# Where a layer's merge gates run: eight of sixteen moved from the Mamba stage to the end of the HGRN2 heads

## The chip, the cores and the metric

One core of a Trainium2 chip runs the whole program in one launch. The metric is device microseconds, the median of several executions.

## What is computed

One layer of a streaming encoder for two groups of requests that share the weights: a prompt of 512 tokens, and 8 sampled streams of 16 tokens. Normalised and modulated tokens `h` go through one wide projection, and its parts feed two mixers side by side, a gated linear attention (HGRN2) and a state space model (Mamba-2). Two of the parts, `ga` and `gb`, gate the mixers' outputs:

```python
proj = h @ w_in
q_r, f_r, i_r, g_r, z, xbc, dt_r, ga_r, gb_r = jnp.split(proj, cuts, axis=-1)
...
o = (_rms(o) * hg_norm_w.astype(f32).reshape(HG_HEADS, HG_DV)).reshape(bn, t, HG_WIDTH)
o = (o * jax.nn.silu(g_r.astype(f32))).astype(h.dtype)
pa = o @ w_branch_a
...
pb = y @ w_branch_b
merged = jax.nn.sigmoid(ga_r) * pa + jax.nn.sigmoid(gb_r) * pb
```

`ga` and `gb` have 1024 columns each, so they are sixteen column blocks of 128. Behind the mixers come `w_out`, a second norm and an expert channel mixer (PEER), which takes the larger part of the time and is not touched by the change.

## The kernel before

The tokens are worked on in two passes that share weight loads: A (names that end in A; the first 128 prompt tokens and the 128 sampled ones, 256 columns) and B (384 prompt tokens). Values lie transposed, channels on partitions. A projection of one block of 128 output channels is float32 made of three matmuls per block of 128 input channels (`mm3`, L265): `wsplit` (L255) loads 512 KB of weights as `raw` on SP's queue, ScalarE rounds it to `whi` and VectorE takes the rest as `wlo`; then 24 matmuls of 128x256 (pass A) go to one PSUM bank of the kind `pj`. There are four such banks, three banks `sm` for everything else, and one `ad`. The rings of the weights have 5 (`raw`) and 4 (`whi`, `wlo`) buffers.

The stages, in the order of the program:

- `hgrn_in` (L572): four head pairs. Each has its V projections for both passes (L588), three projections for each of its two heads and both passes (`projs`, L295), and then `hgrn_head` (L626) for pass A's two heads: the levels of the attention (L649), the state (L672), the sample streams (L686, L698), and at the end the output: a copy to the tile `oT` (L704), its square, a column sum on TensorE, Ln and Exp for the norm (L312, L313), two multiplications (L708 and the one ahead of it) and a store (L709). `oT` has two buffers in the pool of this stage. After the third pair the dt projections of both passes are made (`steps_all`).
- `mamba_in` (L806): first GA = 4 gates, then four groups. A group (`mamba_out`, L833) has six projections with convolutions (ScalarE copies the bank to `xp`, L784) and four for z, then `mamba_group` (L853): transposes, the state (L892) and outputs, a norm at the end. Behind each group come GG = 3 gates.
- `merge` (L969) loads the gates and both mixers' outputs back from DRAM.

A gate (`gate`, L827) is one projection, a Sigmoid on ScalarE into the tile `stGA` (two buffers, in a pool that is opened when the heads are through) and a store to `g_sp` on ScalarE's queue. The change touches the constants GA and GG, `hgrn_in`, `mamba_in` and `gate`.

`projs` also advances a generator (`step`, L308) that spreads the rest of the ada projections (the conditioning, L495: four matmuls a step into the `ad` bank; L501 puts the finished result in place) over the projections of these stages.

The program is written in this order, but each engine's order is then set by the framework's scheduler, which simulates the program and may move an instruction ahead of others on its engine:

```python
with tile.TileContext(nc, schedule_with_timeline_sim=True) as tc, ExitStack() as ctx:
```

So an instruction of a later stage can stand among those of an earlier one, where its tiles and banks allow it.

Of the kernel before, what the change touches and what calls it, by code (L numbers as in the profile page):

```python
# [8 lines left out]
F32 = mybir.dt.float32  # L9
# [8 lines left out]
P = 128  # L18
# [110 lines left out]


LATE = 0
GA = 4
GG = 3
GS = 0
L2 = 10
L3 = 0
# [54 lines left out]
class Kernel:  # L191
# [380 lines left out]
    def hgrn_in(self, md):  # L572
        nc, I, V, A, PE, lb, (p, q) = self.nc, self.I, self.V, self.A, self.PE, self.lb, self.passes
        with self.pool("gpA") as gp:
            tg = lambda w: lambda name, bufs=2, shape=None: gp.tile(shape or [P, w.W], F32, name=name + w.name, bufs=bufs)
            ta, tb = tg(p), tg(q)
            for hpair in range(4):
                vsb = ta("vsb", 2, [P, 2, 256]), tb("vsb", VB, [P, 3, 256])
                wv = [self.wsplit(I["w_v"][hpair, s]) for s in range(2)]
                for w, vs in zip(self.passes, vsb):  # L580
                    for t in range(w.nt):
                        ps = self.pj()
                        n = 0
                        for k in range(KD):
                            vh_, vl_ = wv[k // 4]
                            ks = slice((k % 4) * 256, (k % 4 + 1) * 256)
                            for a, b in ((w.H[1], vh_), (w.H[0], vh_), (w.H[0], vl_)):
                                PE.matmul(ps[:, :256], a[:, k, t * P:(t + 1) * P], b[:, ks], start=n == 0, stop=n == 23)  # L588
                                n += 1
                        A.activation(vs[:, t, :], ps[:, :256], AF.Copy)  # L590
                nc.scalar.dma_start(self.spill["v"][hpair], vsb[1])
                heads = []
                for s in range(2):
                    h = 2 * hpair + s
                    kq = ta("kq", 4, [P, 4, p.W]), tb("kq", 2, [P, 4, q.W])
                    for w, o, ps, t_ in zip(self.passes, kq, self.projs(I["w_in"][h], self.passes), (ta, tb)):
                        t1 = t_("t1")
                        A.activation(t1, ps, AF.Sigmoid)
                        V.tensor_mul(o[:, 1, :], t1, ps)
                    for w, o, ps, t_ in zip(self.passes, kq, self.projs(I["w_in"][8 + h], self.passes), (ta, tb)):  # L600
                        t1, t2 = t_("t1"), t_("t2")
                        A.activation(t1, ps, AF.Sigmoid)
                        A.activation(t2, ps, AF.Sigmoid, scale=-1.0)
                        V.tensor_scalar(o[:, 0, :], t2, lb[:, 1, h:h + 1], None, OP.mult)
                        A.activation(t1, t1, AF.Ln, bias=lb[:, 0, h:h + 1], scale=lb[:, 1, h:h + 1])
                        V.tensor_tensor_scan(o[:, 2, :], self.smask(w), t1, 0.0, OP.mult, OP.add)
                    for w, o, ps, t_ in zip(self.passes, kq, self.projs(I["w_in"][16 + h], self.passes), (ta, tb)):
                        t1 = t_("t1")
                        A.activation(t1, ps, AF.Sigmoid)
                        V.tensor_mul(o[:, 3, :], t1, ps)  # L610
                    nc.scalar.dma_start(self.spill["kq"][h], kq[1])
                    heads.append((h, kq[0], vsb[0][:, :, s * P:(s + 1) * P]))
                for h, kq, vh in heads:
                    self.hgrn_head(p, ta, h, kq, vh)
                if hpair == STP:
                    self.steps_all(md)

# [188 lines left out]
    def mamba_in(self, md):  # L806
        nc, I, O, (p, q) = self.nc, self.I, self.O, self.passes
        with self.pool("gtA") as sp:
            p.hist, q.hist = md.tile([P, 24, 8, 3], F32, name="hist"), None
            nc.scalar.dma_start(p.hist, I["hist"])  # L810
            p.cnv, q.cnv = md.tile([P, 24, 8, 3], F32, name="cnvA"), self.md.tile([P, 24, 1, 3], F32, name="cnvB")
            gates = list(range(16))

            def more(n):
                for _ in range(min(n, len(gates))):
                    j = gates.pop(0)
                    self.gate(self.passes if j < GS else self.passes[:1], sp, j)

            more(GA)
            with self.pool("mcA") as p.mc, self.pool("mpA") as mp:  # L820
                for g in range(4):
                    self.mamba_out(p, mp, mp, g)
                    more(GG)
                more(16)
            nc.scalar.dma_start(O["conv_s"], p.cnv)

    def gate(self, passes, sp, j):  # L827
        for p, ps in zip(passes, self.projs(self.I["w_in"][64 + j], passes)):
            st = sp.tile([P, p.W], F32, name="stG" + p.name, bufs=2)
            self.A.activation(st, ps, AF.Sigmoid)  # L830
            self.nc.scalar.dma_start(p.g_sp[j], st)

# [574 lines left out]
```

## Time and profile before

| | |
|---|---|
| median of 3 runs | 2904.71 us (2904.02 to 2907.4) |
| the profiled execution | 2904.54 us |
| its span | 2902.7 us |
| TensorE's mean granted clock | 0.966 |
| heads and Mamba stage of pass A | some 290 to 680 us of the span |

In the rows below PE is TensorE's matmul, PEld its weight loading, DVE VectorE, ACT ScalarE, POOL GpSimd and SP the queue of SyncE; ACTq and SPq are an engine's instructions that only issue DMAs. L830 is line 830 of the kernel. `pj<-hlA,whi` reads: written to `pj`, read from `hlA` and `whi`. A bracket at a row's end is the idle time of the engine before it, and what ended it. A row of windows has the stretch, its length, the busy time of PE, PEld, DVE, ACT and POOL with the number of instructions, then PE's granted clock, the DMA share and GB/s. The clock is a share of full speed, 1.00 being 2.4 GHz and 0.50 1.2 GHz.

### The profile page before, as it was taken

How to read it: one execution, taken by the hardware profiler on the slowest of the kernel's cores; microseconds unless marked ns; L12 is line 12 of the kernel's file. 1: busy time of each engine (PE TensorE's matmuls, PEld its weight loads, DVE VectorE, ACT ScalarE, POOL GpSimd, SP SyncE). 2: the span in 40 equal slices, each digit the busy share in tenths (PEclk: the TensorE clock that was granted, in tenths of full speed). 3: DMA queues.
4: the chain of work that ended last, by engine and by line, in shares of the span. 5: the costliest groups of instructions: out<-in, count | busy, mean ns of one | idle time of the engine just before them, and what ended most of it. 6: DMA issues, size and time to landing. Idle time of an engine off the chain costs nothing. (4 is left out here: it accounts for less than half of the span.)

```text
span 2902.7 us, 41739 instructions
## 1 busy us (share of the span) xinstructions
PE 2697.5 (93%) x15177; PEld 2258.9 (78%) x15177; DVE 2132.2 (73%) x4364; ACT 1344.4 (46%) x2056; POOL 731.8 (25%) x682
## 2 busy tenths in 40 slices
PE   6999989998989999977898998997999999999998
PEld 3988868777877555645897777896878999999997
DVE  4556748777778778776788897775667777777776
ACT  3667647764532355644334244554333333333334
POOL 0000002000000443331353476300124444333330
PEclk8999989999999999988998999998999999999999
DMA  8344456657534787666798698967889888888984
GB/s 298 122 150 157 141 181 213 211 175 269 186 115 128 259 293 267 240 218 222 288 330 329 235 338 324 329 224 275 273 285 324 302 313 299 306 302 308 306 303 155
DMA packets 274150, 725.14 MB, mean 250 GB/s; under 512 B 25456, under 2 KB 112760, under 8 KB 270488
## 3 DMA queue, kind: packets, MB, share of 16 engines
q1 hardware_dynamic: 153144, 348.50, 35.7%
q0 software_dynamic: 73920, 269.66, 26.5%
q10 hardware_dynamic: 46880, 104.32, 9.9%
q8 instruction: 119, 1.95, 0.3%
q14 instruction: 87, 0.71, 0.1%
HBM read 646.36 MB, written 76.02 MB: 249 GB/s over the span
## 5 line engine op out<-in xcount | busy, mean ns | idle before, releaser
L1195 POOL DMA_INDIRECT row<-in_u,eidx x256 | 336.5, 1315 | 973.8 <-DVE row L1200 519.8
L1200 DVE SCALAR_TENSOR_TENSOR row<-row,h2t 128x1024 f32<-128x1024 f32 x256 | 307.6, 1220 | 48.1 <-DMA row<-in_u,eidx 47.7
L1294 PE MATMUL po<-vl,wh 128*128 128x512 f32 x768 | 301.0, 392 | 18.8 <-ACT wh L1348 15.2
L289 PE MATMUL pj<-h,raw 128*128 128x384 f32 x896 | 305.2, 495 | 3.2 <-ACT xpB L784 2.3
L1294 PE MATMUL po<-vh,wh 128*128 128x512 f32 x768 | 301.6, 393 | 0.0
L1294 PE MATMUL po<-vh,wl 128*128 128x512 f32 x768 | 299.8, 391 | 0.0
L261 ACT ACTIVATE whi<-raw 128x1024 fp32r<-128x1024 f32 (+1 forms) x169 | 176.5, 1049 | 222.2 <-PE pj L273 135.8
L289 PEld LDWEIGHTS pj<-h,raw 128*128 128x128 f32 x896 | 170.0, 194 | 116.5 <-issue 8.1
L253 DVE TENSOR_TENSOR wlo<-raw,whi 128x1024 fp32r<-128x1024 f32 (+1 forms) x169 | 204.9, 1215 | 63.7 <-ACT whi L261 62.2
L1256 ACT ACTIVATE uh<-ur 128x1024 fp32r<-128x1024 f32 x128 | 135.8, 1061 | 241.9 <-PE s L1264 228.0
L253 DVE TENSOR_TENSOR ul<-ur,uh 128x1024 fp32r<-128x1024 f32 x128 | 156.5, 1222 | 98.7 <-ACT uh L1256 98.5
L1264 PE MATMUL s<-h2h,ul 128*128 128x384 f32 x672 | 225.6, 336 | 0.0
L1264 PE MATMUL s<-h2l,uh 128*128 128x384 f32 x672 | 225.4, 335 | 0.0
L1264 PE MATMUL s<-h2h,uh 128*128 128x384 f32 x672 | 225.1, 335 | 0.0
L1195 POOL DMA_INDIRECT row<-in_v,eidx x128 | 151.2, 1182 | 277.7 <-DVE acc L1210 253.4
L273 PE MATMUL pj<-hlA,whi 128*128 128x256 f32 x648 | 194.0, 299 | 11.2 <-ACT stGA L830 4.9
L273 PE MATMUL pj<-hhA,wlo 128*128 128x256 f32 x648 | 191.4, 295 | 1.6 <-DVE wlo L253 1.6
L273 PE MATMUL pj<-hhA,whi 128*128 128x256 f32 x648 | 191.2, 295 | 0.0
L1294 PEld LDWEIGHTS po<-vl,wh 128*128 128x128 f32 x768 | 145.0, 189 | 49.9 <-ACT wh L1348 15.4
L253 DVE TENSOR_TENSOR vl<-vr,vh 128x1024 fp32r<-128x1024 f32 x128 | 158.5, 1240 | 22.5 <-ACT vh L1306 22.5
L1306 ACT ACTIVATE vh<-vr 128x1024 fp32r<-128x1024 f32 x128 | 135.0, 1056 | 83.7 <-PE po L1294 83.2
L1294 PEld LDWEIGHTS po<-vh,wl 128*128 128x128 f32 x768 | 144.1, 188 | 30.3
(482 smaller groups left out, 7005.6 us busy)
## 6 DMA issues: line engine op xcount, KB each, us to landing
raw<-in_w_in SPq DMA_DIRECT2D x136, 512.0 KB, 4.4
ur<-in_uT SPq DMA_DIRECT2D x128, 512.0 KB, 6.5
vr<-in_vP SPq DMA_DIRECT2D x128, 512.0 KB, 5.8
raw<-in_w_ada SPq DMA_DIRECT2D x48, 512.0 KB, 5.2
g_d<-gt ACTq DMA_DIRECT2D x24, 1024.0 KB, 6.7
gm<-g_d SPq DMA_DIRECT2D x48, 512.0 KB, 7.1
raw<-in_w_b SPq DMA_DIRECT2D x32, 512.0 KB, 5.7
raw<-in_w_q SPq DMA_DIRECT2D x32, 512.0 KB, 4.7
```

The costliest lines, as they stand in the source:

```text
L253: self.V.tensor_tensor(out, raw, hi.bitcast(F32), OP.subtract)
L261: self.A.activation(hi[:, :n], raw[:, :n], AF.Copy)
L273: self.PE.matmul(ps[:m, :W], a[:, k * m:(k + 1) * m], b[:, k0 + k, :], start=start and q == 0, stop=stop and q == 3 * nk - 1)
L289: self.PE.matmul(ps[:, :W], raw[:, k * P:(k + 1) * P], x[:, k, :], start=k == 0, stop=k == KD - 1)
L1195: self.paced(self.G.indirect_dma_start(out=r, out_offset=None, in_=src, in_offset=bass.IndirectOffsetOnAxis(ap=at, axis=0)), pin)
L1200: self.paced(V.scalar_tensor_tensor(r, r, 1.0, self.h2t[:, n, :], OP.mult, OP.mult, accum_out=act[:, s:s + 1]), pin)
L1256: A.activation(uh, ur, AF.Copy)
L1264: PE.matmul(ps[:, :W], a[:, k, :], c[:, k, :], start=q == 0, stop=q == 3 * KD - 1)
L1294: PE.matmul(po[n][hf], a[:, ts], c[:, ds], start=b == 0 and q == 0, stop=b == P - 1 and q == 2)
L1306: A.activation(vh, vr, AF.Copy)
```

## The change

Of the sixteen gates of pass A, eight are now traced in `hgrn_in`, two behind each of heads 4 to 7 (GH = 2), and are staged in the head's own `oT` tiles. No gate stands ahead of the Mamba groups any more (GA = 0), and two instead of three stand behind each group (GG = 2).

```diff
@@ -129,8 +129,9 @@
 
 
 LATE = 0
-GA = 4
-GG = 3
+GA = 0
+GG = 2
+GH = 2
 GS = 0
 L2 = 10
 L3 = 0
@@ -612,6 +613,8 @@
                     heads.append((h, kq[0], vsb[0][:, :, s * P:(s + 1) * P]))
                 for h, kq, vh in heads:
                     self.hgrn_head(p, ta, h, kq, vh)
+                    for j in range(GH * (h - 4), GH * (h - 3)) if h >= 4 else ():
+                        self.gate(self.passes[:1], None, j, lambda: ta("oT"))
                 if hpair == STP:
                     self.steps_all(md)
 
@@ -809,7 +812,7 @@
             p.hist, q.hist = md.tile([P, 24, 8, 3], F32, name="hist"), None
             nc.scalar.dma_start(p.hist, I["hist"])
             p.cnv, q.cnv = md.tile([P, 24, 8, 3], F32, name="cnvA"), self.md.tile([P, 24, 1, 3], F32, name="cnvB")
-            gates = list(range(16))
+            gates = list(range(4 * GH, 16))
 
             def more(n):
                 for _ in range(min(n, len(gates))):
@@ -824,9 +827,9 @@
                 more(16)
             nc.scalar.dma_start(O["conv_s"], p.cnv)
 
-    def gate(self, passes, sp, j):
+    def gate(self, passes, sp, j, out=None):
         for p, ps in zip(passes, self.projs(self.I["w_in"][64 + j], passes)):
-            st = sp.tile([P, p.W], F32, name="stG" + p.name, bufs=2)
+            st = out() if out else sp.tile([P, p.W], F32, name="stG" + p.name, bufs=2)
             self.A.activation(st, ps, AF.Sigmoid)
             self.nc.scalar.dma_start(p.g_sp[j], st)
 
```

Lines of the changed kernel are one further from the constants on, and three further behind `hgrn_in`. Its order differs at three places that matter here. The numbers in the names only tell buffers apart.

First ScalarE at the end of head 7. In the order before, the head's output copy, its norm and its stores come first, then the two first gates (`stGA`, out of the banks `pj_3909` and `pj_3947`):

```order
L704 ACTIVATE oTA_3883<-sm_3855 128x256
L705 ACTIVATE osqA_3884<-oTA_3883 128x256
L312 ACT_TABLE_LOAD
L312 ACTIVATE orsA_3885<-sm_3888,eps_77 128x256
L313 ACT_TABLE_LOAD
L313 ACTIVATE orsA_3885<-orsA_3885 128x256
L702 DMA out_hg_s<-S0A_3856 128x1024
L709 DMA o_spA_95<-oTA_3883 128x256
L830 ACT_TABLE_LOAD
L830 ACTIVATE stGA_3938<-pj_3909 128x256
L830 ACTIVATE stGA_3976<-pj_3947 128x256
```

Of the change, the same place:

```order
L707 ACTIVATE oTA_4111<-sm_4083 128x256
L833 ACT_TABLE_LOAD
L833 ACTIVATE oTA_4158<-pj_4129 128x256
L708 ACTIVATE osqA_4112<-oTA_4111 128x256
L834 DMA g_spA_97<-oTA_4158 128x256
L833 ACTIVATE oTA_4196<-pj_4167 128x256
L834 DMA g_spA_97<-oTA_4196 128x256
L705 DMA out_hg_s<-S0A_4084 128x1024
L313 ACT_TABLE_LOAD
L313 ACTIVATE orsA_4113<-sm_4116,eps_77 128x256
L314 ACT_TABLE_LOAD
```

The gates' Sigmoids have moved ahead of the norm's Ln and Exp, two stores to `g_spA` stand between, and the second Sigmoid writes an `oT` tile.

Then TensorE at head 7. Before: the head's last levels, its state and outputs, the column sum of its norm, and then the first projection of the Mamba stage, `pj_4070`:

```order
L649 MATMUL sm_3832<-lvcA_3826 128x128 x2
L327 MATMUL sm_3846<-con_72,ktA_3838 128x128 x2
L672 MATMUL sm_3851<-vsbA_3056,khatA_3845 128x128
L686 MATMUL sm_3855<-qtA_3837,S0A_3856 128x16 x8
L687 MATMUL sm_3855<-attA_3757,vsbA_3056 128x128
L690 MATMUL sm_3855<-attA_3757,vsbA_3056 128x128
L698 MATMUL sm_3870<-veA_3868,khatA_3845 128x512
L698 MATMUL sm_3876<-veA_3868,khatA_3845 128x512
L319 MATMUL sm_3888<-osqA_3884,ones_75 128x256
L501 MATMUL sm_4327<-con_72,raw_4325 128x128 x4
L273 MATMUL pj_4070<-hlA_111,whi_4065 128x256
```

Of the change, the first of Mamba's projections is `pj_4222`:

```order
L274 MATMUL pj_4222<-hlA_111,whi_4217 128x256
L274 MATMUL pj_4222<-hhA_110,whi_4217 128x256
L320 MATMUL sm_3902<-osqA_3898,ones_75 128x256
L274 MATMUL pj_4222<-hhA_110,wlo_4218 128x256
L274 MATMUL pj_4222<-hlA_111,whi_4217 128x256
L274 MATMUL pj_4222<-hhA_110,whi_4217 128x256
L637 MATMUL sm_3986<-kqA_3562 128x128 x2
L274 MATMUL pj_4222<-hhA_110,wlo_4218 128x256
L274 MATMUL pj_4222<-hlA_111,whi_4217 128x256
L274 MATMUL pj_4222<-hhA_110,whi_4217 128x256
L274 MATMUL pj_4222<-hhA_110,wlo_4218 128x256
```

Its matmuls now stand with the column sum of head 6's norm (L320) and the first matmul of head 7 (L637), ahead of head 7's levels. Three more of Mamba's projections follow among head 7's matmuls and beside its norm.

Last TensorE at the end of head 4. Before, the head's state and outputs stand among the V projections of the last pair (`pj_3096`):

```order
L672 MATMUL sm_2696<-vsbA_2030,khatA_2690 128x128
L686 MATMUL sm_2700<-qtA_2682,S0A_2701 128x16 x8
L687 MATMUL sm_2700<-attA_2602,vsbA_2030 128x128
L690 MATMUL sm_2700<-attA_2602,vsbA_2030 128x128
L698 MATMUL sm_2715<-veA_2713,khatA_2690 128x512
L588 MATMUL pj_3096<-whi_3059,hlA_111 128x256
L588 MATMUL pj_3096<-whi_3059,hhA_110 128x256
L588 MATMUL pj_3096<-wlo_3060,hhA_110 128x256
L588 MATMUL pj_3096<-whi_3059,hlA_111 128x256
L588 MATMUL pj_3096<-whi_3059,hhA_110 128x256
L698 MATMUL sm_2721<-veA_2713,khatA_2690 128x512
```

Of the change:

```order
L675 MATMUL sm_2696<-vsbA_2030,khatA_2690 128x128
L689 MATMUL sm_2700<-qtA_2682,S0A_2701 128x16 x8
L690 MATMUL sm_2700<-attA_2602,vsbA_2030 128x128
L693 MATMUL sm_2700<-attA_2602,vsbA_2030 128x128
L701 MATMUL sm_2715<-veA_2713,khatA_2690 128x512
L496 MATMUL ad_2516<-raw_2985,cs_80 32x512
L701 MATMUL sm_2721<-veA_2713,khatA_2690 128x512
L496 MATMUL ad_2516<-raw_2985,cs_80 32x512
L274 MATMUL pj_2998<-hlA_111,whi_2993 128x256
L274 MATMUL pj_2998<-hhA_110,whi_2993 128x256
L274 MATMUL pj_2998<-hhA_110,wlo_2994 128x256
```

Gates (`pj_2960` just ahead of these rows, and `pj_2998`) and an ada step (L496) have come between, and the V projections stand behind them.

## Rows read from the trace of the kernel before

**Rows 1.** Page, part 1: busy us (share of the span) and instructions

```profile
PE 2697.5 (93%) x15177; PEld 2258.9 (78%) x15177; DVE 2132.2 (73%) x4364; ACT 1344.4 (46%) x2056; POOL 731.8 (25%) x682
```

**Rows 2.** Page, part 4: chain that ended last, by engine

```profile
PE 24%; DMA 1%; DVE 1%; issue 0%; ACT 0%; SPq 0%; DVEq 0%; ACTq 0%
```

**Rows 3.** Windows of 75 us (length, busy per engine, clock, DMA share, GB/s)

```profile
300.00:375.00 75.00, 73.41 (x481) 63.34 (x480) 50.41 (x130) 50.12 (x75) 0.00 (x0) 0.98 0.41 137
375.00:450.00 75.00, 60.46 (x378) 50.80 (x377) 36.26 (x110) 38.61 (x67) 6.02 (x20) 0.83 0.60 196
525.00:600.00 75.00, 73.01 (x528) 61.28 (x529) 64.89 (x137) 53.45 (x93) 7.79 (x31) 0.98 0.70 222
```

**Rows 4.** Windows of 10 us around head 7, same columns

```profile
390.00:400.00 10.00, 7.28 (x41) 3.27 (x40) 5.77 (x12) 4.15 (x6) 0.00 (x0) 1.00 0.72 224
400.00:410.00 10.00, 6.63 (x24) 5.44 (x25) 6.98 (x27) 3.75 (x7) 0.00 (x0) 0.50 0.56 220
410.00:420.00 10.00, 8.46 (x32) 6.33 (x30) 2.98 (x11) 3.99 (x6) 0.64 (x6) 0.64 0.07 14
420.00:430.00 10.00, 6.63 (x40) 6.64 (x41) 0.91 (x2) 2.98 (x6) 0.00 (x0) 0.66 0.76 233
```

**Rows 5.** Timeline of TensorE at head 7 (start, us, line, idle before)

```profile
398.81 1.05 PE L495 MATMUL ad<-raw,cs 128*32 128x512 f32 x4 [2.23 <-DMA raw<-in_w_ada]
...
410.03 3.43 PE L686 MATMUL sm<-qtA,S0A 128*128 128x16 f32 x16
...
417.87 0.60 PE L501 MATMUL sm<-con,raw 128*128 128x128 f32 x4
...
423.37 0.58 PE L273 MATMUL pj<-hlA,whi 128*128 128x256 f32 x1 [4.90 <-ACT stGA L830]
```

**Rows 6.** Timeline of ScalarE at head 7 and Mamba's first group

```profile
414.54 0.39 ACT L704 ACTIVATE oTA<-sm 128x256 f32<-128x256 f32 x1 [5.15 <-PE sm L690]
...
418.56 1.28 ACT L313 ACT_TABLE_LOAD   x1
419.85 0.42 ACT L313 ACTIVATE orsA<-orsA 128x256 f32<-128x256 f32 x1
...
422.93 0.66 ACT L830 ACTIVATE stGA<-pj 128x256 f32<-128x256 f32 x2
...
427.71 0.39 ACT L830 ACTIVATE stGA<-pj 128x256 f32<-128x256 f32 x1 [4.12 <-DMA g_spA<-stGA]
...
465.57 0.38 ACT L830 ACTIVATE stGA<-pj 128x256 f32<-128x256 f32 x1
```

**Rows 7.** Timeline of TensorE, an ada step and a projection

```profile
341.48 1.05 PE L495 MATMUL ad<-raw,cs 128*32 128x512 f32 x4
342.46 0.39 PE L273 MATMUL pj<-hlA,whi 128*128 128x256 f32 x1
...
345.42 0.34 PE L273 MATMUL pj<-hlB,whi 128*128 128x384 f32 x1
```

**Rows 8.** Line L704, the four last heads' output copies

```profile
L704 ACT ACTIVATE oTA<-sm x4: 367/384/385, 294.1 to 414.5; 128x256 f32<-128x256 f32 x4
```

**Rows 9.** Page, part 5: the two instructions that split a weight tile

```profile
L261 ACT ACTIVATE whi<-raw 128x1024 fp32r<-128x1024 f32 (+1 forms) x169 | 176.5, 1049 | 222.2 <-PE pj L273 135.8
L253 DVE TENSOR_TENSOR wlo<-raw,whi 128x1024 fp32r<-128x1024 f32 (+1 forms) x169 | 204.9, 1215 | 63.7 <-ACT whi L261 62.2
```

**Rows 10.** Timeline of TensorE at the boundary of two Mamba groups

```profile
524.99 0.44 PE L327 MATMUL sm<-con,xTg 128*128 128x128 f32 x2 [2.51 <-ACT btok L863]
...
534.39 1.02 PE L892 MATMUL sm<-xw,btok 128*128 128x512 f32 x2
```

**Rows 11.** Timeline of TensorE, the merge's first projection

```profile
682.92 0.39 PE L273 MATMUL pj<-ol,whi 128*128 128x256 f32 x1 [4.71 <-DVE ol L253]
```

**Rows 12.** Tile stGA, its stores

```profile
DMA to landing us min/median/max: 1.7/3.9/5.0
```

**Rows 13.** Timeline of VectorE at the boundary

```profile
535.44 0.69 DVE L894 COPY Hs<-sm 128x512 f32<-128x512 f32 x1 [0.34 <-PE sm L892]
```

## The prediction

> **What bounds the kernel now.** I read the page first. TensorE is busy for 93% of the span and VectorE for 73% [rows 1], so in most places an instruction taken off TensorE's stream, or an idle stretch filled on it, is what can change the time. The chain of waits says nothing on the place of the change: followed back from the end it covers 28% of the span, nearly all of it late TensorE work [rows 2]. So the stage itself has to be looked at, in windows. From 300 to 375 us, where the last head pair's projections run and heads 4 and 5 lie, TensorE is busy for 73.41 of 75 us at a granted clock of 0.98; from 525 to 600, in the Mamba stage, for 73.01 at 0.98; but from 375 to 450, between them, for 60.46 at 0.83 [rows 3]. Those 75 us hold heads 6 and 7 and the start of the Mamba stage: the hole.
>
> Cut in tens, the hole is plain: from 400 to 430 the granted clock is 0.50, 0.64 and 0.66, and busy time 6.63 to 8.46 of each 10 us, with 0.50 the lower level of 1.2 GHz [rows 4]. TensorE was half idle before the clock fell: head 7 runs bare there, a chain through VectorE and ScalarE for which TensorE has short matmuls only. TensorE's timeline shows what it holds: an ada step (four matmuls) that first waits 2.23 us for its weights, then the head's own matmuls, then 4.90 us of nothing before Mamba's first projection, until ScalarE has read a gate out of its bank [rows 5]. That wait is the key. ScalarE's timeline tells why it is so long: head 7's output is copied at 414.54, its norm takes two table loads until 419.85, and the two Sigmoids come at 422.93, a third only at 427.71, after 4.12 us of waiting for the first store to land [rows 6]. The gates' matmuls were done long before; all four projection banks were held by finished gates.
>
> **The change part by part.** The number of gates is sixteen before and after, so the sum is about where they run. In the order before, the first four gates already stand among heads 6 and 7 on TensorE, and only their Sigmoids wait for the end of the heads. Of the eight gates after, four take that place, four go behind heads 4 and 5, and each Mamba group loses one. The four banks then come free at heads 6 and 7, and four Mamba projections move up under head 7.
>
> One projection for this pass is 24 matmuls: from 342.46 to the next one's start at 345.42, 2.96 us [rows 7].
>
> 1. *Four gates behind heads 4 and 5.* The first output copy in the list, head 4's, lies at 294.1 [rows 8], and TensorE is full from there on [rows 3]: 4 x 2.96 = +11.8 us, nothing covers them. Each gate holds a bank until its Sigmoid, which stands behind the head's output copy on ScalarE, and the second of a pair also waits for the landing of the first one's store, because the tile is one of two that the head itself uses. With two banks held and a third by the dt projection of the other pass, the projections behind can wait. Not in the trace; bounds 0 (enough other work is queued) and two waits like today's 4.90, 9.8 [rows 5]. I take +2, near zero, since here the heads run beside projections and ScalarE is busy two thirds of the time only (50.12 of 75) [rows 3].
>
> 2. *Ada steps.* Every projection also moves the ada work on by a step, and eight gates in place of four use up five of its steps earlier, so that five leave head 7's hole for a stretch where TensorE is full. One is 1.05 us [rows 7]: 5 x 1.05 = +5.2. Its cover was the hole; bounds +2.6 (half of it had cost time there too: one waited 2.23 for its weights [rows 5]) and +5.2.
>
> 3. *End of the heads and first Mamba group.* Before, the first ten projections of Mamba run from 423.37 [rows 5] to the first of its gates: that Sigmoid starts at 465.57 [rows 6], so the ten end at 465.57 - 2.96 = 462.6; 39.2 us for 29.6 of work. After, four of them are done in head 7's hole, and the fifth can start once ScalarE gets to the first conv copy. From the output copy at 414.54: a table load 1.28, a gate's Sigmoid 0.39, the square about 0.4 (an estimate by the Sigmoid of the same size), a landing 4.1, the other Sigmoid 0.39, the norm's two loads and two operations of 0.42, 3.4, and two weight splits that stand between, 2 x 1.05 [rows 6, 9]: 426.6. With the hole filled the clock should be higher and the head's own matmuls shorter, so I take 425. Then six projections, 17.8, and 2 for small waits: 444.8, or -17.8. Bounds: -21.4 (start at 423.4, no wait) and -8 (the fifth starts 6 us later, since a landing wait comes twice, and the six keep today's pace of 3.92 each: 454.6).
>
> 4. *Mamba's groups lose a gate each.* 4 x 2.96 = -11.8 if TensorE sets the pace there. The window 525 to 600 says so (73.01 against 64.89 for VectorE [rows 3]). Bound from the other side: -4.9, if it is VectorE, whose share of a gate is one split of 1.215 [rows 9].
>
> 5. *Cover lost at the last group's end.* The gates behind a group are what TensorE does while that group's normalisation and the next one's transposes are waited for. At the boundary from 524.99 on it idles 2.51 us in spite of three gates, and the matmul that fills the state comes at 534.39 [rows 10]. With two gates some of that opens. Bounds 0 and the whole stretch, 9.4; I take +4, more than one gate's 2.96, since in the order after, group 3's block stands right behind two gates.
>
> 6. *Merge.* Its first projection waits 4.71 us for the split of the head outputs [rows 11]; their reloads now stand ahead of the last norm. I take -3; bounds -4.7 (all of it goes) and +4 (the gates' loads for the merge come later among SP's loads, a landing late).
>
> 7. *ScalarE.* The order has 11 more table loads (two at the heads, nine in Mamba), 11 x 1.28 = 14.1 us, and four more waits for a landing, of 4.1 each (median landing 3.9) [rows 6, 12], with evacuations queued behind them. ScalarE is busy for 53.45 of 75 us in Mamba [rows 3], so I count zero beyond what step 3 holds; if that cover is gone it is rival C. The load at 418.56 takes 1.28 and the next operation starts at 419.85, that is at once [rows 6]. The Trainium skill, in "ScalarE: Activation LUTs", section "What ACT_TABLE_LOAD costs", adds a drain of about 1.38 us, some 2.66 us for each change of table; 11 of them would be an estimated 29 us of ScalarE. The row shows no drain; by the page rival C would be dearer, by the row it is not.
>
> 8. *DMAs.* The same sixteen stores leave on ScalarE's queue and the same 512 KB weight loads on SP's; only their places change. DMA is busy for 0.41 from 300 to 375 [rows 3], so eight more weight loads there find room: nothing.
>
> Sum: +11.8 + 2 + 5.2 - 17.8 - 11.8 + 4 - 3 = -9.6. The profiled execution took 2904.54, 0.17 under the median of 2904.71, which is nothing here: **2895.0**.
>
> **The rivals.** *A, the Mamba stage is paced by VectorE.* Then step 4 gives only 4.9: -9.6 + 6.9 = -2.7, 2902. For it: VectorE is busy for 64.89 of 75 us there [rows 3]. Against it: at the boundary VectorE's copy at 535.44 waits for TensorE, not the other way round [rows 13]. Chance 0.20.
>
> *B, slower: the banks pile up at heads 4 and 5.* Place: the last pair's projections, right behind head 4's and head 5's output. If at each of the two heads the projections wait once for a Sigmoid (4.9 as today) and once for a landing (4.1), that is 2 x 9.0 = 18 in place of 2: -9.6 + 16 = +6.4, 2911. It decides when more than about 12 us of new waits stand there. For it: the wait of 4.90 is exactly of this kind, and ScalarE's queue is in order, so a landing wait holds up every evacuation behind it. Against it: four banks, of which two stay in use. Chance 0.17.
>
> *C, ScalarE comes onto the path.* The table loads and landing waits delay the evacuations in Mamba, whose copies TensorE waits for: +14.1, -9.6 + 14.1 = +4.5, 2909. For it: ScalarE's order is fixed, and the nine loads lie between conv copies. Against it: 21 us of idle in 75. Chance 0.08.
>
> *D, the change does less than it says.* Four of the eight gates stand where they stood; if their banks come free no earlier (the landing wait at head 7 takes the place of the 4.90), step 3 shrinks to -8: +0.2, 2905. Chance 0.05.
>
> **How the numbers follow.** Forecast 0.50, A 0.20, B 0.17, C 0.08, D 0.05. A measurement of this kernel tells a difference of about 0.2%, 5.8 us, from no change, so faster means under 2898.9 and slower over 2910.5. The forecast with its bounds is faster but for a tenth of its cases; A with step 3 or 6 at their good ends is so too in part; B is slower, and the worse part of C. Faster 0.53, within 0.26, slower 0.21. The range has at its low end step 3 at -21.4 and steps 1, 5 and 6 at their good ends in part, 2884; at its high end B, 2912.
>
> **What would show it.** Right: no 4.90 us of waiting for a gate before Mamba's first projection; four Mamba projections on TensorE before head 7's norm; clock from 400 to 430 back near 1.0 (2.4 GHz); the stretch around heads 4 and 5 longer by 17 to 20 us, Mamba shorter. Wrong in step 1: waits for gates' Sigmoids in the last pair's projections. Wrong in step 4: the Mamba groups shorter by less than 2.96 each, with TensorE idle for VectorE or ScalarE inside them. Wrong in step 5: idle time at the group boundaries of far more than 4. The forecast as a whole is wrong if new waits in heads 4 and 5 and in Mamba exceed about 10 us together.

## The result, and the profile after

The changed kernel is slower: 2928.51 us against 2906.06 in the first comparison, ratio 1.0074 (95% interval 1.0058 to 1.0091). Run twice more, it gave 1.0084 (1.0063 to 1.0104) and 1.0070 (1.0050 to 1.0090). The forecast was 2895, and the range ended at 2912. Executions of one kernel differ by 10 to 20 us, so what follows rests on several profiles of each.

The page of the changed kernel, part 1, answers to [rows 1]: the same work, 6 us more of TensorE's busy time, 16 more of ScalarE's, and a longer span (2928.3 us).

```profile
PE 2703.7 (92%) x15177; PEld 2261.2 (77%) x15177; DVE 2132.7 (73%) x4364; ACT 1360.7 (46%) x2067; POOL 732.7 (25%) x682
```

The hole at head 7 was filled in part. The 10-us windows of the changed kernel there (columns as in [rows 4]; head 7's output lies at 439.8 now):

```profile
410.00:420.00 10.00, 10.00 (x66) 7.23 (x66) 4.69 (x17) 3.56 (x8) 0.00 (x0) 1.00 0.24 74
420.00:430.00 10.00, 7.61 (x61) 7.17 (x61) 6.57 (x21) 7.00 (x9) 0.00 (x0) 1.00 0.62 187
430.00:440.00 10.00, 6.94 (x38) 6.26 (x37) 6.04 (x13) 2.97 (x6) 0.08 (x1) 0.79 0.61 214
440.00:450.00 10.00, 9.60 (x58) 7.51 (x56) 3.08 (x11) 6.60 (x10) 0.57 (x6) 0.87 0.38 134
```

The clock is at 0.79 or above, where it was 0.50 to 0.66 [rows 4], and the 4.90 us of waiting for a gate [rows 5] is gone; TensorE still stands idle for 5.5 us between head 6's output and head 7's (6.1 before). New waits stand elsewhere. The list of TensorE's waits from 280 to 720 us (total, times, longest), changed kernel:

```profile
PE pj L274 <- DVE x L999: 12.0, 1, 12.0
PE sm L328 <- ACT btok L866: 6.2, 2, 5.1
PE sm L328 <- DVE xt L882: 5.3, 1, 5.3
...
PE sm L763 <- ACT dtac L752: 4.4, 1, 4.4
```

The same list of the kernel before has no wait over 4.9:

```profile
PE sm L327 <- ACT btok L863: 6.0, 2, 3.4
PE pj L273 <- DVE ol L253: 4.9, 2, 4.7
PE pj L273 <- ACT stGA L830: 4.9, 1, 4.9
```

To see where the time went, take the starts of a few instructions that both kernels have, and the stretches between them: means over three profiles of the kernel before and four of the changed one, with differences of the unrounded means (one of each is of the kernel with a barrier behind pass B's merge, described below; up to there its order is the same). In brackets is what the forecast's steps make of them.

| stretch (us) | before | changed | difference |
|---|---|---|---|
| head 3's output copy to head 5's | 73.6 | 79.4 | +5.8 |
| head 5's to head 6's | 72.1 | 88.9 | +16.8 (both together: +19.0, steps 1 and 2) |
| head 6's to head 7's | 21.1 | 24.1 | +2.9 |
| head 7's to the first conv copy | 16.2 | 11.5 | -4.7 |
| first conv copy to the fourth z copy | 29.7 | 26.1 | -3.7 (the three together: -17.8, step 3) |
| fourth z copy to the first group's state | 11.0 | 9.7 | -1.2 |
| first group's state to the fourth's | 183.6 | 177.0 | -6.7 |
| fourth's to the merge's first multiplication | 35.0 | 40.0 | +5.0 |
| first to eighth multiplication | 22.3 | 19.9 | -2.4 (the four together: -10.8, steps 4 to 6) |
| sum | | | +11.9 (forecast: -9.6) |

So about half of the loss arises up to the end of pass A's merge. The forecast expected nothing behind it; there the other half is.

### The profile page after: what moved, and what is told of

It reads as the page before. It is cut to its first block, busy times and chain, and to the rows that moved or that the text cites. A ratio compares the mean times of both kernels' runs of the same rounds, so it can differ in the third digit from the quotient of the medians.

```text
span 2928.3 us, 41717 instructions
## 1 busy us (share of the span) xinstructions
PE 2703.7 (92%) x15177; PEld 2261.2 (77%) x15177; DVE 2132.7 (73%) x4364; ACT 1360.7 (46%) x2067; POOL 732.7 (25%) x682
## 4 chain that ended last, share of the span: by engine, by line
PE 59%; DVE 11%; DMA 11%; issue 10%; ACT 5%; POOL 3%; ACTq 0%; SPq 0%; DVEq 0%; POOLq 0%
PE po L1297 15%; PE s L1267 12%; PE pj L274 11%; PE pj L1267 5%; PE pj L290 3%; POOL row L1198 3%; DMA row<-in_u,eidx 3%; PE sm L1245 3%; DMA w<-s_d 2%; PE ga L1187 2%; PE pj L589 1%; DVE row L1203 1%; PE sm L652 1%; PE ad L496 1%; DMA raw<-in_w_ada 1%
## 5 line engine op out<-in xcount | busy, mean ns | idle before, releaser
L262 ACT ACTIVATE whi<-raw 128x1024 fp32r<-128x1024 f32 x169 | 176.5, 1049 | 194.0 <-PE pj L274 147.0
L254 DVE TENSOR_TENSOR wlo<-raw,whi 128x1024 fp32r<-128x1024 f32 x169 | 205.2, 1219 | 56.4 <-ACT whi L262 55.9
L274 PE MATMUL pj<-hlA,whi 128*128 128x256 f32 (+1 forms) x648 | 193.1, 298 | 5.4 <-DVE xs L796 3.8
L274 PE MATMUL pj<-hhA,whi 128*128 128x256 f32 (+1 forms) x648 | 192.1, 296 | 0.0
L274 PE MATMUL pj<-hhA,wlo 128*128 128x256 f32 (+1 forms) x648 | 189.7, 293 | 0.8 <-DVE wlo L254 0.8
```

The lines of the kernel that those rows point to most:

```text
L254: self.V.tensor_tensor(out, raw, hi.bitcast(F32), OP.subtract)
L262: self.A.activation(hi[:, :n], raw[:, :n], AF.Copy)
L274: self.PE.matmul(ps[:m, :W], a[:, k * m:(k + 1) * m], b[:, k0 + k, :], start=start and q == 0, stop=stop and q == 3 * nk - 1)
```

## The experiments

Every kernel was timed in turn with the kernel before on its chip; a ratio is to that.

**The two halves of the change.** Gates behind heads 6 and 7 only, with GG = 3 (`late_only`):

```diff
-GG = 2
+GG = 3
...
-  for j in range(GH * (h - 4), GH * (h - 3)) if h >= 4 else ():
+  for j in range(GH * (h - 6), GH * (h - 5)) if h >= 6 else ():
...
-  gates = list(range(4 * GH, 16))
+  gates = list(range(2 * GH, 16))
```

> Two gates behind heads 6 and 7 only, three behind each Mamba group as before, none behind heads 4 and 5. Theory 1 (the loss comes from the four gates at heads 4 and 5 and from what the Mamba groups lose by having two gates instead of three; freeing the four banks at heads 6 and 7 is a gain in itself): heads 4 to 6 as before, head 7's output at 414.5 within 3 us, the first Mamba group's state 8 to 12 us earlier than before's 471.6, no new wait at the merge, total 2893 to 2899. Theory 2 (the banks freed early give nothing: what ScalarE has to do between head 7's output and the first conv copy is 12 us either way, and Mamba's projections wait for that): first group's state within 3 us of before, total 2903 to 2910.

Measured: 1.0023 (1.0011 to 1.0035), 2913.0 against 2907.1. Head 7's output came at 417.2, the first group's state at 472.1 (471.6 in the first profile of before). Theory 1 falls: freeing the banks brings nothing by itself. The total lies even over theory 2's, by 3 us. From the first conv copy to the fourth z copy this kernel took 30.9 us, though two of Mamba's projections stand ahead of head 7's output.

Gates behind heads 4 and 5 only, with GA = 4 and GG = 2 (`early_only`: the loop is `if 4 <= h < 6`, the list begins at `2 * GH`):

> Two gates behind heads 4 and 5 each, four ahead of the Mamba groups as before, two behind each group. Theory 1: the four gates cost 20 to 25 us at the heads (before against changed kernel: head 6's output 392.6 to 415.6), nothing comes back at head 7, three groups give back 12, the last group and the merge lose 10 to 15 as in the changed kernel (12.0 us wait for the gates' load): 5 to 12 us slower than the changed kernel, 2933 to 2941. Theory 2: nothing was gained at head 7 by the changed kernel, so this one takes the same time as it, 2926 to 2931.

Measured: 1.0099 (1.0080 to 1.0118), 2938.9. That is 4 to 8 us over the changed kernel's three ratios, whose intervals it overlaps. As theory 1 said: head 6's output at 415.2, and from the fourth group's state to the merge's first multiplication 39.6 us, as in the changed kernel.

**The price of a gate at heads 4 and 5.** The kernel before, and four gates computed a second time (`early_twice`):

```diff
+  self.gdup = self.dram.tile([4, P, 2 * P], F32, name="gdup")
...
+  for j in range(GH * (h - 4), GH * (h - 3)) if 4 <= h < 6 else ():
+      self.gate(self.passes[:1], None, j, lambda: ta("oT"), self.gdup)
...
```

(`gate` stores to the tensor that it is given.)

> The kernel before with four gates more, computed a second time behind heads 4 and 5 and stored to a scratch tensor that nobody reads; sixteen gates stay where they were. Measures what four gates cost there. Theory 1: head 6's output is 20 to 25 us later than before's 392.6 (12 for the matmuls, 5 for ada steps that leave head 7's hole, the rest waits), and that stays to the end but for the ada steps: 2921 to 2931. Theory 2 (TensorE has room there, and the cost in the changed kernel came from the order of the rest): head 6's output less than 15 us later, total 2910 to 2920.

Measured: 1.0106 (1.0086 to 1.0125), 2933.5, 2.5 over theory 1's range. Head 6's output came at 414.9, 22.3 us later than in the first profile of before, and the merge's eighth multiplication 25.7 us later. Four gates cost 5.6 us each there, ada steps included, not the 2.96 of a projection. TensorE's waits of this kernel from 280 to 480 us show that none of them waits for a gate of heads 4 and 5; the dt work waits instead:

```profile
PE sm L653 <- DVE lvcA L650: 7.1, 3, 3.5
PE pj L274 <- ACT stGA L834: 4.9, 1, 4.9
PE sm L764 <- ACT dtac L753: 4.5, 1, 4.5
```

**Where the merge waits.** SP's timeline of the changed kernel shows the gates' load late, behind reloads of Mamba's outputs that wait for the last group's stores; ScalarE's shows those stores at 693.76; and VectorE's what waits for the load:

```profile
696.51 1.24 SPq L985 DMA_DIRECT2D st<-y_spA  x2
697.88 0.92 SPq L993 DMA_DIRECT2D x<-g_spA  x2
```

```profile
693.76 0.33 ACTq L969 DMA_DIRECT2D y_spA<-zt  x1
```

```profile
704.16 1.08 DVE L999 TENSOR_TENSOR x<-x,pj 128x256 f32<-128x256 f32 x3 [6.76 <-DMA x<-g_spA]
```

Three finished projections of the merge are multiplied at once at 704.16: until then TensorE waited 12.0 us for a bank. In the kernel before the same load stands behind four of these reloads, here behind eleven; there the first multiplication comes at 688.3. Two edits move one of the parties to GpSimd's queue. First the gates' load (`gate_load_queue`):

```diff
-  nc.sync.dma_start(dst[:, j:j + 4, :], p.g_sp[n + j:n + j + 4].rearrange("m p w -> p m w"))
+  nc.gpsimd.dma_start(dst[:, j:j + 4, :], p.g_sp[n + j:n + j + 4].rearrange("m p w -> p m w"))
```

> The changed kernel with the merge's loads of the gates issued by GpSimd in place of SP, where they stand behind loads that wait for the last Mamba group's stores. Theory 1 (the 12.0 us that TensorE waits in the merge come from that place in SP's queue): the wait falls to under 4 us and the total to 2917 to 2922. Theory 2 (the load waits for the memory that the last group's matmuls free, so that another queue brings little): wait of 9 us or more, total 2925 to 2931.

Measured: 1.0043 (1.0028 to 1.0059), 2920.1, a total within theory 1's figures, but not by its mechanism: the merge's first multiplication was no earlier (709.4). The wait has another name, as TensorE's waits from 440 to 740 us tell:

```profile
PE sm L637 <- DMA kq<-sp_kq: 16.3, 1, 16.3
```

The order had put pass B's first head there, and its load is now the one behind SP's reloads. Then the reloads themselves (`y_reload_queue`):

```diff
-  (nc.sync if RQ else nc.scalar).dma_start(st, src)
+  (dq or (nc.sync if RQ else nc.scalar)).dma_start(st, src)
-  reload(y_sp[k], yh[0], yl[0], k)
+  reload(y_sp[k], yh[0], yl[0], k, nc.gpsimd if p.sample else None)
```

and the same for the second half.

> The changed kernel with pass A's reloads of the Mamba outputs issued by GpSimd in place of SP, so that the merge's loads of the gates, and those of pass B's first head, no longer stand behind loads that wait for the last group's stores. Theory 1 (that place in SP's queue makes the 12.0 us wait in the merge; with the gates' load on another queue only the next load behind it became late): the wait falls under 3 us, the first multiplication of the merge comes at 690 to 696 instead of 704.2, total 2916 to 2922. Theory 2 (whatever is moved, the merge waits for the last group): first multiplication after 700, total 2925 to 2931.

Measured: 1.0050 (1.0035 to 1.0066), 2916.3, where the changed kernel had 1.0084 in the same comparison. The load is issued at 688.30 and the first multiplication comes at 695.1, as theory 1 said, but the wait is down to 7.8 only, not under 3:

```profile
688.30 0.99 SPq L993 DMA_DIRECT2D x<-g_spA  x2
```

```profile
PE pj L274 <- DVE x L999: 7.8, 1, 7.8
```

The place in SP's queue made some 4 of the 12 us. The rest stays: with none of the reloads ahead of it on SP the load still left at 688.30 only and took until 695 to land. By the order it waits for TensorE there, for memory that the last group still uses; that wasn't tried by itself.

**The ends of the groups.** The eight Mamba gates dealt out 1, 2, 2, 3 (`last_group_three`: `more((1, 2, 2, 3)[g])`):

> The changed kernel with its eight Mamba gates dealt out 1, 2, 2, 3 in place of 2, 2, 2, 2. Theory 1 (with few gates the scheduler draws the next group's projections ahead, four of them by the last group, so that the last one has nothing left to run beside; a third gate there covers it): from the third to the fourth group's state 54 us or more instead of 50.1, but to the merge's eighth multiplication 4 to 8 us less in all, total 2920 to 2925. Theory 2 (what the last group gains the first one loses): total 2926 to 2931.

Measured: 1.0065 (1.0043 to 1.0087), 2923.8 against 2902.8; the changed kernel had 1.0084 in the same comparison. The intervals overlap, and inside it the parts went otherwise than expected: 49.4 us from the third to the fourth group's state, 64.7 from there to the merge's eighth multiplication (59.9 in the changed kernel). The wait for the gates' load was 7.8 here as well, but 5.8 us of waits for weights had come. It decides nothing.

All gates in Mamba, four a group, GA = 0 and GG = 4 (`all_in_mamba`, made from the kernel before):

> No gate behind heads or ahead of the groups, four behind each Mamba group; by its order four Mamba projections then run beside heads 6 and 7 in the place of the gates. Theory 1 (a projection that ScalarE evacuates for the convolution fills the hole at head 7 as well as a gate, costs no table load there, and a fourth gate covers the group boundaries): first conv copy at or before 425 (430.6 before), fourth group's state no later than before's 653.5, total 2893 to 2903. Theory 2 (what stands behind head 7 is a chain on ScalarE and VectorE that no filling shortens, as with gates behind heads 6 and 7 only): fourth group's state 653 to 658, total 2905 to 2914.

Measured: first conv copy at 420.7, fourth group's state at 641.0, the merge's eighth multiplication at 702.0, where the three executions of before have 705.1 to 716.1. Up to there theory 1 holds, though in the shortest of this kernel's twelve executions. The total does not follow: 2908.7, 1.0020 (1.0003 to 1.0038), as theory 2 had it.

**What paces the first Mamba group.** From the first conv copy to the fourth z copy the kernel before, `late_only` and `all_in_mamba` all take 29.5 to 30.9 us, with none, two and four of Mamba's first ten projections ahead of head 7's output copy; the changed kernel, with two, takes 26.1. At the first conv copy about two are done in the kernel before and four in each of the others. Windows of that stretch, of a second profile of the kernel before, then of `all_in_mamba`, `late_only` and the changed kernel:

```profile
426.00:455.00 29.00, 25.67 (x213) 25.31 (x212) 21.05 (x49) 27.08 (x52) 10.85 (x23) 1.00 0.64 208
```

```profile
420.00:451.00 31.00, 24.99 (x178) 23.98 (x178) 17.88 (x50) 27.81 (x53) 6.51 (x26) 0.89 0.61 200
```

```profile
428.00:460.00 32.00, 23.89 (x183) 23.49 (x184) 19.92 (x55) 25.77 (x53) 8.51 (x26) 0.92 0.68 221
```

```profile
452.00:478.00 26.00, 22.91 (x179) 22.70 (x179) 19.24 (x51) 22.29 (x49) 8.81 (x26) 0.93 0.69 243
```

ScalarE, the fourth pair of numbers, is busy for 27.08 of 29 and for 27.81 of 31 us, in the first at TensorE's full clock too. It evacuates, convolves and splits weights. In none of these four stretches does it wait for a matmul, while TensorE waits 3.1 to 4.6 us for `xs`, that is for a bank which the convolution hasn't read yet. So TensorE isn't what is waited for.

Work done ahead does take its weight splits off ScalarE: between the two copies it makes ten in the kernel before and six in the other three. Its table loads differ as well, four before, three in the changed kernel, seven in `all_in_mamba`. That leaves it busy for 27.6, 21.8 and 27.2 us, and the stretch follows this, not the number of finished projections. In `late_only` it is busy for 24.7 only and waits 5.0 us for weights. This is read from traces; taking work off ScalarE by itself wasn't tried.

**The other half: behind the merge.** The profiles behind pass A's merge show small differences everywhere: the scheduler ordered pass B and the expert mixer anew, though the diff doesn't touch them. A barrier of all engines takes that away: behind it the kernel before and the changed one have the same instructions in the same order on every engine.

```diff
   x2, sq, pp = self.merge(p)
+  self.tc.strict_bb_all_engine_barrier()
```

The changed kernel once more came ahead of it, to see how far executions of one order differ (`changed_again`):

> The changed kernel once more, for a second profile. From the merge's eighth multiplication to the end the first profile took 2204.5 us, before's 2191.5. Theory 1 (the rest of the kernel got another order on its engines, and that costs 10 us): 2201 to 2208 again. Theory 2 (executions differ by that much): anything from 2188 to 2209, most likely nearer 2195.

Measured: median 2927.4, but the profiled execution was the shortest of its six (2914.55): 719.3 to the eighth multiplication, and 2193.5 from there, 11 us less than in the first profile, as theory 2 allows. One profile can't settle it. So the barrier, on before, changed and `all_in_mamba`:

> The kernel before with one barrier of all engines behind pass A's merge. The two kernels with this barrier have the same instructions in the same order on every engine behind it, which the two without it have not. It's the reference of the next three; the barrier itself should cost 3 to 15 us, from what now overlaps there: 2906 to 2920.

> The changed kernel with the same barrier. Theory 1 (the change costs 8 to 13 us up to the end of the merge, as both its profiles say, and the other 10 of the measured 22 to 24 come from another order of what follows): 8 to 13 us over the kernel before with the barrier. Theory 2 (the whole difference is made up to the merge, and the two profiles are not typical): 18 us or more over it. Theory 3 (a shift alone makes the same instructions behind it slower): also 18 or more, but with the profile showing 8 to 13 at the barrier.

> The kernel with all sixteen gates in the Mamba stage, four a group, with the same barrier; its order behind the barrier is nearly that of the other two. Theory 1 (it gains 9 us up to the end of the merge, and without the barrier loses them to another order of the rest): 6 to 11 us under the kernel before with the barrier. Theory 2 (its gain up to the merge is that of one lucky execution): within 3 us of it.

Measured, on one chip: 2952.8, 2962.6 and 2946.3. The changed kernel is 9.8 us over before, all gates in Mamba 6.5 under it: medians that lie within theory 1's figures both times, and that fit the stretches up to the merge. But each kernel has five or six executions that spread over 16 to 23 us, and the intervals of the ratios overlap (1.0134, 1.0108 to 1.0160, for before; 1.0167, 1.0141 to 1.0194; 1.0107, 1.0083 to 1.0132). The barrier alone costs 39 us (2913.8 without it), far over what was expected, so it changes more than the order; that it hides a part of the loss can't be excluded.

A fourth one kept the ada steps out of the moved gates (`no_ada_steps_cut`; `projs` calls `self.step()` only where asked):

> The changed kernel with the barrier, where the eight gates behind the heads do not advance the ada work, which then stays with the other projections. Leaves nothing out. If the prediction's second step is right (ada steps that moved out of head 7's hole cost 5 us where TensorE is full), head 6's output comes 4 to 6 us earlier than in the changed kernel (413.9 and 415.6 there), and of this 2 to 5 us are left at the barrier. If they cost nothing there, head 6's output is within 2 us of the changed kernel's.

Measured: 2966.2, 3.7 over the changed kernel with the barrier, with intervals that overlap. Head 6's output came at 407.3, against 412.0 to 415.6 in the changed kernel's profiles. From head 3's output to head 6's this kernel takes 159.8 us, the changed one 168.0 to 168.5 (166.5 with this barrier) and the one before 145.7 in the mean: at the heads the steps cost 6.7 to 8.7 us, somewhat more than step 2 said. Nothing of it was left at the merge's eighth multiplication (718.7 against 715.8), where 2 to 5 us were expected: they were owed again in Mamba.

The same barrier behind pass B's merge:

> The kernel before with the barrier of all engines behind pass B's merge, in the middle of the program, in place of pass A's. Reference of the next one: 2906 to 2945.

> The changed kernel with the barrier behind pass B's merge; behind it both kernels have the same order, ahead of it their own. If the second half of the loss comes from the order of pass B's heads, groups and merge: 18 to 25 us over the kernel before with this barrier. If it comes from the order of the expert mixer, or from executions: 8 to 13 us over it, as with the barrier behind pass A's merge.

Measured: 2933.2 and 2944.0, 10.9 us apart (1.0068, 1.0047 to 1.0090, and 1.0113, 1.0091 to 1.0134), the second of the two expectations: with the same expert mixer the change costs some 11 us, with its own 19 to 25. But the two profiles put the 11 us elsewhere than the first barrier did. Up to the eighth multiplication the changed kernel is 8.4 us later; from there to pass B's merge it takes 669.6 us against 658.2; from pass B's merge to the end 1541.2 against 1553.2, 12 us less, some 10 of them behind the barrier, where the order is the same. A second profile of before and a third of the changed kernel looked at that last stretch:

> The kernel before, unchanged, for a second profile. From pass B's merge (its first multiplication) to the end its first profile took 1524.7 us; the changed kernel's two took 1535.1 and 1529.0. If the other half of the loss lies in the order of the expert mixer: 1522 to 1528 again. If it's chance: most likely 1529 or more.

> The changed kernel for a third profile, on the same chip as the second one of the kernel before. If the order of the expert mixer costs: 1530 to 1537 from pass B's merge to the end. If it's chance: anything from 1522 to 1537. Up to the eighth multiplication of pass A's merge 719 to 725 either way.

Measured from pass B's merge to the end: before 1524.7 and 1527.5, changed 1535.1, 1529.0 and 1532.2. Both came out where an effect of the order would put them. But the mean difference is 6 us, not 11, the two kernels' values lie 1.5 us apart at the nearest, and with one order behind a barrier two executions have just been seen some 10 us apart. So these profiles don't show an effect of the expert mixer's order. The unchanged kernel against itself gave 0.9985 (0.9968 to 1.0002) there, medians 7 us apart, so a part of the rest can be chance.

Last, whether the gain of all gates in Mamba shows where the rest has the same order. With the gates' load on GpSimd's queue its order behind pass A's merge is nearly that of before with that queue:

> The kernel before with the merge's loads of the gates on GpSimd's queue. Theory 1 (the order of the rest, which this edit changes too, decides by itself over 10 us): up to the merge's eighth multiplication 5 to 12 us later than before (as with the changed kernel, where pass B's first head then waited for its loads), total anywhere within 15 us of before. If only what stands up to there counts, total 2910 to 2917.

> All sixteen gates in the Mamba stage, four a group, and the merge's loads of the gates on GpSimd's queue. Behind pass A's merge it has nearly the same order as the kernel before with that queue. Theory 1 (four Mamba projections under head 7 and a fourth gate behind each group are worth 6 to 9 us, and show in the time where the rest has the same order): 5 to 10 us under the kernel before with that queue. Theory 2 (the gain doesn't outlast the rest of the program): within 3 us of it.

Measured: 2921.8 (ratio 1.0035, 1.0021 to 1.0049) and 2918.3 (1.0011, 0.9998 to 1.0024): 3.5 us apart, between the two theories, with intervals that overlap. The queue alone costs the kernel before 9 us (2912.6), within what theory 1 of the first expectation allowed. At the merge's eighth multiplication the gain doesn't show in this pair (719.0 us with all gates in Mamba, in the longest of its twelve executions, against 716.3). None of the kernels beat the one before.

## Why the prediction was wrong

*Steps 1 and 2, gates and ada steps at heads 4 and 5:* +19.0 forecast, +22.6 measured, within the bounds. The kernel without ada steps in the moved gates parts the two. It takes 159.8 us from head 3's output to head 6's, 14.1 over the kernel before: step 1, the gates, was right (+13.8). The steps make the other 8.5 (6.7 against the changed kernel with the same barrier), where step 2 had 5.2. Four steps leave head 7's hole, not five (16 of the 20 `ad` matmuls between head 6's output and head 7's), and they come early. The +5.8 up to head 5's output are seven steps more (44 `ad` matmuls in place of 16), with no more projections than before; without the steps that stretch takes 73.9, as before. The matmuls of the four gates stand in the +16.8 behind it, together with 5.5 us more of idle time. That isn't banks that pile up (rival B), since no wait for a gate stands there, but in the main the dt work: `dtac` is late, since ScalarE waits 5.94 us for VectorE's `q` ahead of it, TensorE waits 4.42 us at 375.19, and its granted clock is 0.79 over the 15 us from 375 on (1.00 in the kernel before). B had the sign of the outcome, but neither the mechanism nor the size: 16 us over the sum at this place, where 3.6 were measured.

*Step 3 is the step that failed:* -17.8 forecast, -5.4 measured, short of its bound of -8. Its chain on ScalarE was right in sum, as ScalarE's timeline at head 7 shows:

```profile
439.85 0.38 ACT L707 ACTIVATE oTA<-sm 128x256 f32<-128x256 f32 x1 [4.78 <-PE sm L693]
440.25 1.28 ACT L833 ACT_TABLE_LOAD   x1
441.54 0.38 ACT L833 ACTIVATE oTA<-pj 128x256 f32<-128x256 f32 x1
...
451.81 0.26 ACT L787 ACTIVATE xpA<-pj 128x128 f32<-128x128 f32 x1
```

12.0 us from the output copy to the first conv copy, where 12.1 were worked out (the wait for the landing was 1.44 in place of 4.1, other waits made up for it). Wrong was what came next: "then six projections, 17.8, and 2 for small waits", 19.8 us as if TensorE set the pace from there on. To the fourth z copy it was 26.1, of which ScalarE is busy for 21.8 and never waits for a matmul: the path runs over ScalarE and the convolution that it shares with VectorE, and of their work the four finished projections take away little but the weight splits. The rows of before left room for this: 39.2 us for 29.6 of work stood there, and ScalarE's share of that stretch wasn't looked at. Besides, head 7 itself became 2.9 us longer with more work beside it, where the sum had counted on a shorter one. The -5.4 are near rival D's -8, which had a chance of 0.05, but D's reason doesn't hold: the banks did come free, and the 4.90 went.

Two readings of the forecast were off besides: the ten projections didn't last until 462.6, since ScalarE copies the bank of the last one at 460.65, and the chain of [rows 2] covers some 26% of the span, not 28%. Neither decides anything.

*Steps 4 to 6:* -10.8 forecast, -5.3 measured. The groups gave 6.7 and 1.2 where three gates less are 8.9, so step 4 was nearly right, and rival A's 1.2 a gate too little; the last group and the merge lost 2.6 on balance where about 2 were to be won (its own gate, the cover and the wait for `ol` together). Cover was lost, as step 5 said: from 640 us on TensorE waits 5.3 us for `xt` in the last group, where the kernel before waits 3.4 for `btok`. Step 6 had the bound for the gates' load coming late (+4), and the point value ignored it; the wait of 4.71 [rows 11] went, and one of 12.0 took its place.

*Step 7, ScalarE's 14 us of table loads:* the load at 440.25 takes 1.28, and the Sigmoid behind it starts at 441.54, at once, so no drain is in the sum. The Trainium skill, in "ScalarE: Activation LUTs", section "What ACT_TABLE_LOAD costs", has one of about 1.38 us at each change of table. By that rule the chain of 12.0 us, with its three loads, would be an estimated 4 us longer; the trace doesn't agree with it. The four waits for a landing behind the heads took 5.6 us together, not 4.1 each. What the nine loads in Mamba cost wasn't tried by itself.

*What was in no step:* that the rest of the program, nearly 2200 us that the diff doesn't touch, is ordered anew. By the medians with a barrier it makes about half of the loss: 9.8 and 10.9 us are left of 19 to 25. With five or six executions each that is no more than a rough half, and a barrier costs 21 to 39 us itself. In which part of the program the half lies stays open: the medians point at the expert mixer, the profiles with the second barrier don't.

## What to carry to other kernels

An idle stretch of the busiest engine is worth filling only if that engine also paces what follows: look at the busy time of the others in the next stretch first, and at what they wait for, since work done ahead waits in its bank for the engine that reads it. The work that is moved is paid at the new place at more than its matmuls, 5.6 us for one of 2.96 here, because what each call drags along (ada steps, a later dt, a clock that drops) comes too; without the ada steps it was 3.5. Where a scheduler orders the program by simulated times, compare orders far behind the change as well, and time a local change with a barrier behind it in both kernels, often enough: here the barrier cost as much as the change or more, and five or six executions left the intervals touching.

## What was not expected of the hardware

Two executions of the changed kernel, with the same instructions in the same order, differ by 11 us between the same two instructions (2204.5 and 2193.5 us), and TensorE's mean granted clock was 0.963 in the first and 0.967 in the second. The two profiles with a barrier behind pass B's merge differ by some 10 us behind it, again in the same order. A barrier of all engines behind pass A's merge cost 39 us, one behind pass B's 21 (2933.2 against 2912.6), where 3 to 15 were expected from what overlaps there; what makes up that price stays open.
